# A hybrid decoder layer on one core: 128 bytes of padding behind the constants, and nine projections instead of eight in the second RWKV loop, the last of them behind the next stage's loads

## The chip, the core and the metric

The kernel runs on one core of one Trainium2 chip. The metric is the device time of one execution in microseconds, as the median of several runs. The core has five engines that run side by side, each with its own queue of instructions: TensorE (matmuls; PE in the profile, and PEld for its weight loads), VectorE (DVE), ScalarE (ACT), GpSimd (POOL) and SyncE (SP, which only issues DMAs here).

## What is computed

One layer (depth 1) over 1024 positions of width 1024, in float32. The normalised input goes through one projection of 3840 columns, and its columns feed three mixers side by side:

```
z = rmsnorm(h, norm_mix_g) @ w_in
h = h + concat[ hgrn2_mix (4 heads x 128), dilated_window_mix (4 heads x 64), rwkv7_mix (4 heads x 64) ] @ w_out
h = h + conv_glu_ffn(rmsnorm(h, norm_ffn_g), ffn_up, conv, ffn_down)          # d_ff 2816
h = h + sigmoid(rmsnorm(h, norm_ple_g) @ ple_gate) * (p @ ple_proj)
return rmsnorm(h, final_norm_g)
```

HGRN-2 is a gated recurrence with a decay per key channel, worked in chunks; the attention mixes three causal windows of dilation 1, 4 and 16; RWKV-7 is a delta-rule recurrence with its own decay, small gates and a group norm behind it.

## The kernel before, in words

Activations lie transposed, 128 channels on the partitions and 1024 positions along the free axis. A float32 matmul is made of three matmuls on a reduced 32-bit type: both operands are split into a high and a low part, and `mm3` (L139 to L143) issues high x high, high x low and low x high, for two halves of 512 positions. A weight block of 128 x 1024 is loaded by `load_w` (L107), cast to its high part on ScalarE (L116) and reduced to its low part on GpSimd or VectorE (L118). A projection of 128 columns of z is then 8 k blocks of 6 matmuls, 128x128 by 128x512.

There are 30 projections. Eight feed RWKV directly. The other 22 feed HGRN (columns 8 to 23) and attention (24 to 29); they are independent of RWKV and serve as cover for its small, dependent matmuls. Two generators make them:

- `project_rest` works in both RWKV loops. It yields after every k block, accumulates in a PSUM buffer of 1024 columns (tag dp, two buffers), scales it on VectorE (`finish`: L425, L428, L430) and stores the result to DRAM (L419). It asks for the weights of its next projection at k = 3.
- `project_late` works in the HGRN and attention stage. It yields after every half of 512 positions, accumulates in the smaller PSUM buffers (tag mx, four), finishes and stores each half (L448). When it has run out, it allocates the tiles for the split mixer outputs, in the memory of the split inputs.

The order of the 22 is one list, `js`: 8 to 15, 24, 25, 26, 16, 17, 20, 21, 19, 23, 27, 28, 29, 18, 22. `rwkv` runs the two pairs of RWKV heads after each other (p = 0, 1). Each time it takes the next projections from the list by FILL: the first number of a pair is how many are done ahead of the main loop, the second how many are taken in all. `rwkv_main` has 22 turns with one k block each. `rwkv_norm` then runs the group norm of the second half of positions: statistics on VectorE, ScalarE and GpSimd (L694 to L703), then transposes on TensorE (L710), the gate matmul (L714) and the gating on VectorE (L711, L712, which reads bv, L715). It has three steps, and takes up to 6 k blocks behind each. What is left of the generator is drained behind it. With FILL (4, 8) the second loop has 64 blocks: 32 ahead, 22 in the main loop, and 10 in the norm.

The RWKV tiles' memory is then given to the pools of the HGRN and attention stage, and `phase_mix` interleaves four generators there by an order written out by hand, 36 rounds: A (HGRN heads 0 and 2), B (heads 1 and 3, from round 6), C (attention, in the rounds of TURNS) and F (`project_late` with the four projections that are left, in odd rounds up to 15). The first step of A loads f and q of head 0 from DRAM (L458, SyncE's queue); the first step of C loads q, k and v of the first attention half (L458, GpSimd's queue). The attention scores (L1034) go to two dp buffers, one for each of two heads; the values' transposes (L1017) and HGRN's scores (L869, L890) go to mx buffers. The framework sets semaphores by itself, and lets an instruction go ahead of others in its engine's order where it expects its operands earlier.

Memory of the on-chip store is taken from two sides. The left side begins with the constants (parameters, `cst`, and `cmask`, the HGRN masks as one byte per entry, 9 masks x 128 = 1152 bytes per partition); behind them come small tiles, the weight tiles (tags whi, wlo) and then the stages' pools: x0 and x1 with the split activations, ty with three operand sets of the FFN, and others. The right side begins with a tile of 160 bytes that nobody uses (pool edge), then t16 (sixteen operand tiles of 2048 bytes: p1 and p2 of the up phase, the activations of the down phase), ep, px (the embedding's input), and in the last phase x0 (first half of the positions). The large tiles of both sides are whole multiples of 256 bytes, so what comes first on a side sets the place of all that follows, counted within 256 bytes.

The output projection, the FFN (a seven-product scheme for 2x2 blocks: up phase at L1189, 22 units of 7 products; down phase at L1483, 7 products over 11 k) and the last gate follow; the change touches no line of them.

Of the kernel before, what the change touches and what calls it, by code (L numbers as in the profile page):

```python
# [36 lines left out]

CC_ID, CC_BONE, CC_MSK, CC_I64 = 0, 128, 256, 384
NC0 = CC_HG = 448
NCC = CC_HG + 9 * 128  # L40


def shape_constants():
    c = np.zeros((P, NCC), np.float32)
    pp = np.arange(P)[:, None]
    ff = np.arange(P)[None, :]
    c[:, CC_ID:CC_ID + P] = pp == ff
    same = (pp // 64) == (ff // 64)
    c[:, CC_BONE:CC_BONE + P] = same
    f64 = np.arange(64)[None, :]  # L50
    c[:, CC_MSK:CC_MSK + 64] = pp % 64 < f64
    c[:, CC_MSK + 64:CC_MSK + 128] = pp % 64 <= f64
    c[:, CC_I64:CC_I64 + 64] = pp % 64 == f64
    c[:, CC_HG:CC_HG + P] = pp == ff
    for l in range(7):
        n = 1 << l
        c[:, CC_HG + (l + 1) * P:CC_HG + (l + 2) * P] = (pp // n) ^ 1 == ff // n
    c[:, CC_HG + 8 * P:CC_HG + 9 * P] = pp < ff
    u = np.arange(T)[None, :]
    d = pp - (u - 896)  # L60
    cnt = ((d >= 0) & (d <= 128)).astype(np.float64)
    cnt += (d >= 0) & (d <= 512) & (d % 4 == 0)
    cnt += (d >= 0) & (d <= 2048) & (d % 16 == 0)
    sw = np.where(cnt > 0, 8.0 * np.log(np.maximum(cnt, 1.0)), -1e30).astype(np.float32)
    return c, sw


def interleave(order, streams):

    live = dict(streams)  # L70
    while live:
        for s in order:
            if s in live and next(live[s], STOP) is STOP:
                del live[s]


def handover(a, b, steps=14):

    for _ in range(steps):
        next(a)  # L80
        yield
    for i, _ in enumerate(b):
        if i == 1:
            for _ in a:
                yield
        yield
# [5 lines left out]
class Trunk:  # L92
# [183 lines left out]
    def setup(self):  # L276
# [7 lines left out]
        self.id64 = self.cst[:, CC_I64:CC_I64 + 64]  # L284
        self.cmask = cp.tile([P, NCC - NC0], U8, name="cmask")
        few = cp.tile([P, 8], F32, name="few")
# [15 lines left out]
    def load_masks(self, tp):  # L302
        t = tp.tile([P, NCC - NC0], F32, name="ctmp")
        self.nc.gpsimd.dma_start(t, self.a["cst"][:, NC0:])
        self.nc.gpsimd.tensor_copy(self.cmask, t)
# [18 lines left out]
    def phase_mix(self):  # L324
        nc, tc = self.nc, self.tc
        self.mix_norm()
        with tc.tile_pool(name="slots", bufs=1) as slots:
            self.slots, self.NSLOT = slots, 8
            self.rwkv()
        self.O, self.done = None, []  # L330
        for p in (0, 1):
            self.o_split(6 + p)
        with tc.tile_pool(name="hg", bufs=1) as slots, tc.tile_pool(name="sw", bufs=1) as sp:
            self.slots, self.NSLOT = slots, 11
            self.hgrn_setup()
            self.sp = sp
            self.swmask = sp.tile([P, T], F32, name="swmask")
            nc.scalar.dma_start(self.swmask, self.a["swm"])
            A = handover(self.hgrn_head(0), self.hgrn_head(2))
            B = handover(self.hgrn_head(1), self.hgrn_head(3))  # L340
            order = []
            for r in range(36):
                order += "C" * (r in self.TURNS) + "A" + "B" * (r > 5) + "F" * (r % 2 and r < 16)
            interleave(order, {"A": A, "B": B, "C": self.swa(sp), "F": self.project_late(self.rest)})

    TURNS = [i * 33 // 22 for i in range(23)]

    def mix_norm(self):

# [122 lines left out]
    def rwkv(self):  # L472
        nc, tc = self.nc, self.tc
        lt = self.mix_in(0, 6, "lora")
        nc.scalar.activation(lt[0:64, :], lt[0:64, :], AF.Tanh)
        sg = self.mix_in(1, 7, "sg")
        nc.scalar.activation(sg, sg, AF.Sigmoid)
        self.z = {}
        js = iter((*range(8, 16), 24, 25, 26, 16, 17, 20, 21, 19, 23, 27, 28, 29, 18, 22))
        for p in (0, 1):  # L480
            d = {}
            with tc.tile_pool(name=f"pre{p}", bufs=1) as tp:
                self.rwkv_prep(p, tp, lt, d)
                self.rwkv_inverse(p, tp, d)
            lead, n = self.FILL[p]
            fill = self.project_rest([next(js) for _ in range(n)])
            for _ in range(8 * lead):
                next(fill)
            with tc.tile_pool(name=f"rk{p}", bufs=1) as rp:
                self.rwkv_main(p, rp, sg, d, fill)  # L490
            self.rwkv_norm(p, sg, d, 1, fill)
            for _ in fill:
                pass
        self.rest = list(js)

    FILL = (5, 10), (4, 8)

    def rwkv_prep(self, p, tp, lt, d):

# [172 lines left out]

    HALVES = tuple((slice(a, a + 32), slice(a + 32, a + 64)) for a in (0, 64))

    def rwkv_norm(self, p, sg, d, hf, fill):
        for _ in self.rwkv_norm_steps(p, sg, d, hf):
            for _ in range(6):
                next(fill, None)

    def rwkv_norm_steps(self, p, sg, d, hf):  # L680
# [1021 lines left out]
```

## Time and profile before

| | |
|---|---|
| runs of before, us | 1500.29, 1500.64, 1498.69; median 1500.29 |
| the profiled execution | 1501.27 us, of which the span from first to last instruction is 1499.5 |
| mean granted TensorE clock | 0.988 of full speed |
| HBM read, written | 119.95 MB, 46.40 MB (111 GB/s over the span) |
| matmuls on the page | 8910, with as many weight loads |

Times in a row are counted from the span's start. A row of the timeline has start, duration, engine, line, operation and operands; "x2" means that two of a kind were merged. A matmul's duration is modelled and overlaps with its follower's, so a stream's rate is read from start to start. The idle time in brackets is that of the engine just before the instruction, with what ended it.

### The profile page before, as it was taken

How to read it: one execution, taken by the hardware profiler on the slowest of the kernel's cores; microseconds unless marked ns; L12 is line 12 of the kernel's file. 1: busy time of each engine (PE TensorE's matmuls, PEld its weight loads, DVE VectorE, ACT ScalarE, POOL GpSimd, SP SyncE). 2: the span in 40 equal slices, each digit the busy share in tenths (PEclk: the TensorE clock that was granted, in tenths of full speed). 3: DMA queues.
4: the chain of work that ended last, by engine and by line, in shares of the span. 5: the costliest groups of instructions: out<-in, count | busy, mean ns of one | idle time of the engine just before them, and what ended most of it. 6: DMA issues, size and time to landing. Idle time of an engine off the chain costs nothing.

```text
span 1499.5 us, 22728 instructions
## 1 busy us (share of the span) xinstructions
PE 1444.2 (96%) x8910; PEld 1168.8 (78%) x8910; DVE 1062.3 (71%) x1556; ACT 593.2 (40%) x976; POOL 379.8 (25%) x276
## 2 busy tenths in 40 slices
PE   6999999999969999999999999999999999999996
PEld 5778878787857886878778888888888888887885
DVE  6486242782446588646879888888888799767685
ACT  6512221313214445425454444444444444455552
POOL 2221011200112132122034444445554000002332
PEclk9999999999979999999999999999999999999998
DMA  5124012131051211174323333333233883351343
GB/s 215 43 84 135 30 36 93 50 113 58 30 189 64 94 65 41 43 276 167 133 86 112 101 103 106 106 105 98 100 106 118 301 283 92 103 158 57 119 145 123
DMA packets 79739, 167.83 MB, mean 112 GB/s; under 512 B 19920, under 2 KB 22224, under 8 KB 79632
## 3 DMA queue, kind: packets, MB, share of 16 engines
q1 hardware_dynamic: 66176, 146.39, 29.5%
q10 hardware_dynamic: 12368, 15.99, 3.1%
q0 software_dynamic: 1088, 4.00, 0.7%
q8 instruction: 70, 1.15, 0.3%
q14 instruction: 37, 0.30, 0.1%
HBM read 119.95 MB, written 46.40 MB: 111 GB/s over the span
## 4 chain that ended last, share of the span: by engine, by line
PE 48%; issue 2%; DVE 1%; POOL 1%; ACT 0%; DMA 0%; POOLq 0%; ACTq 0%; DVEq 0%
PE bg L1189 15%; PE bv L1189 12%; PE bv L1483 7%; PE bg L1483 7%; PE bv L139 1%; PE bv L141 1%; PE bv L143 1%; PE dp L143 1%; PE dp L141 1%; PE dp L139 1%; PE bg L139 1%; PE bg L141 1%; PE bg L143 1%; POOL wlo L118 0%; POOL rst L192 0%
## 5 line engine op out<-in xcount | busy, mean ns | idle before, releaser
L139 PE MATMUL dp<-xh,whi 128*128 128x512 f32 x544 | 187.9, 404 | 9.4 <-ACT xh L380 9.2
L141 PE MATMUL dp<-xl,whi 128*128 128x512 f32 x544 | 182.5, 395 | 0.8 <-DVE xl L381 0.7
L143 PE MATMUL dp<-xh,wlo 128*128 128x512 f32 x544 | 182.3, 394 | 0.6 <-POOL wlo L118 0.6
L118 POOL TENSOR_TENSOR wlo<-wraw,whi 128x512 fp32r<-128x512 f32 x60 | 81.4, 1356 | 308.1 <-ACT whi L116 279.0
L118 POOL TENSOR_TENSOR wlo<-raw,whi 128x512 fp32r<-128x512 f32 x84 | 135.1, 1627 | 76.2 <-ACT whi L116 76.2
L116 ACT CAST whi<-wraw 128x512 fp32r<-128x512 f32 x120 | 73.3, 618 | 167.7 <-PE dp L141 118.5
L1189 PE MATMUL bg<-t,whi 128*128 128x512 f32 x352 | 135.4, 395 | 0.0
L139 PEld LDWEIGHTS dp<-xh,whi 128*128 128x128 f32 x544 | 99.4, 189 | 33.7 <-ACT xh L380 9.2
L141 PEld LDWEIGHTS dp<-xl,whi 128*128 128x128 f32 x544 | 101.8, 188 | 25.5 <-DVE xl L381 3.1
L143 PEld LDWEIGHTS dp<-xh,wlo 128*128 128x128 f32 x544 | 102.3, 189 | 23.4 <-issue 1.0
L118 POOL TENSOR_TENSOR wlo<-s,whi 128x512 fp32r<-128x512 f32 x44 | 64.4, 1464 | 175.8 <-ACT whi L116 175.8
L1483 PE MATMUL bg<-t,whi 128*128 128x512 f32 x308 | 97.2, 396 | 0.0
L1483 PE MATMUL bv<-t,whi 128*128 128x512 f32 x308 | 96.9, 395 | 0.0
L116 ACT CAST whi<-raw 128x512 fp32r<-128x512 f32 x88 | 52.5, 618 | 95.2 <-issue 48.7
L116 ACT CAST whi<-s 128x512 fp32r<-128x512 f32 x66 | 38.9, 619 | 123.9 <-PE bg L1189 116.1
L1189 PEld LDWEIGHTS bg<-t,whi 128*128 128x128 f32 x352 | 65.9, 187 | 15.8
L192 POOL TENSOR_TENSOR rst<-rst,mhalf 128x4 f32<-128x4 f32 (+1 forms) x9 | 10.3, 1148 | 249.2 <-DVE rst L188 231.6
L1483 PEld LDWEIGHTS bv<-t,whi 128*128 128x128 f32 x308 | 57.8, 188 | 14.0
L118 DVE TENSOR_TENSOR wlo<-wraw,whi 128x512 fp32r<-128x512 f32 x60 | 47.6, 796 | 29.8 <-ACT whi L116 25.1
L1483 PEld LDWEIGHTS bg<-t,whi 128*128 128x128 f32 x308 | 57.7, 188 | 13.9
L1189 PE MATMUL bg<-t,wlo 128*128 128x512 f32 x176 | 68.2, 395 | 0.0
L1479 ACT CAST t<-t 128x512 fp32r<-128x512 f32 x77 | 47.7, 620 | 50.1 <-PE bv L1483 30.4
(402 smaller groups left out, 3502.1 us busy)
## 6 DMA issues: line engine op xcount, KB each, us to landing
raw<-in_ffn_up_dram SPq DMA_DIRECT2D x44, 512.0 KB, 3.5
wraw<-in_w_in_dram SPq DMA_DIRECT2D x30, 512.0 KB, 3.5
z<-zst SPq DMA_DIRECT2D x18, 512.0 KB, 3.2
gb<-ct SPq DMA_DIRECT2D x33, 256.0 KB, 2.2
t<-gb SPq DMA_DIRECT2D x33, 256.0 KB, 2.8
t<-gt SPq DMA_DIRECT2D x33, 256.0 KB, 2.7
zl<-z SPq DMA_DIRECT2D x16, 512.0 KB, 4.0
wraw<-in_ple_gate_dram SPq DMA_DIRECT2D x16, 512.0 KB, 3.4
```

The source lines that it names most:

```text
L116: self.cast = nc.scalar.copy(hi, src).ins
L118: eng.tensor_tensor(lo, src, hi.bitcast(F32), ALU.subtract)
L139: nc.tensor.matmul(ps[hf], wh, xh[hf], start=first, stop=False)
L141: nc.tensor.matmul(ps[hf], wh, xl[hf], start=False, stop=False)
L143: nc.tensor.matmul(ps[hf], wl, xh[hf], start=False, stop=last)
L192: nc.gpsimd.tensor_tensor(r2, r, self.mhalf[:, :n], ALU.pow)
L1189: nc.tensor.matmul(ps, w[part == 2][:, s], X[k][part == 1], start=start and k == part == 0, stop=k == 3 and part == 2, skip_group_check=no ...
L1479: nc.scalar.copy(xh, x)
L1483: nc.tensor.matmul(ps[m], wt[part == 2][:, m * P:(m + 1) * P], (xh, xl)[part == 1], start=k == part == 0, stop=k == NK - 1 and part == 2)
```

## The change

There are two parts. The constants get a tenth block of 128 columns, which stays zero and is used by nobody: `cmask` becomes 1280 bytes wide, and so does the DMA and the cast that fill it.

The second RWKV loop takes nine projections instead of eight (28 comes over from the late ones), 72 blocks: 32 ahead, 22 in the main loop. Its norm takes 3 blocks behind each of its three steps instead of up to 6. The generator is not drained there any more. Its remaining 9 blocks (the last one of projection 27 and all of 28) are a stream M in the next stage, ahead of the rounds, behind the first steps of C and A, which are the loads. TURNS loses its first entry, since that step of C now stands ahead. F has three projections instead of four.

```diff
-NCC = CC_HG + 9 * 128
+NCC = CC_HG + 10 * 128
...
-            order = []
+            order = ["C", "A"] + ["M"] * 24
             for r in range(36):
                 order += "C" * (r in self.TURNS) + "A" + "B" * (r > 5) + "F" * (r % 2 and r < 16)
-            interleave(order, {"A": A, "B": B, "C": self.swa(sp), "F": self.project_late(self.rest)})
-
-    TURNS = [i * 33 // 22 for i in range(23)]
+            interleave(order, {"A": A, "B": B, "C": self.swa(sp), "F": self.project_late(self.rest), "M": self.more})
+
+    TURNS = [i * 33 // 22 for i in range(1, 23)]
...
-            self.rwkv_norm(p, sg, d, 1, fill)
-            for _ in fill:
-                pass
-        self.rest = list(js)
-
-    FILL = (5, 10), (4, 8)
+            self.rwkv_norm(p, sg, d, 1, fill, 6 - 3 * p)
+            if p == 0:
+                for _ in fill:
+                    pass
+        self.rest, self.more = list(js), fill
+
+    FILL = (5, 10), (4, 9)
...
-    def rwkv_norm(self, p, sg, d, hf, fill):
+    def rwkv_norm(self, p, sg, d, hf, fill, n):
         for _ in self.rwkv_norm_steps(p, sg, d, hf):
-            for _ in range(6):
+            for _ in range(n):
                 next(fill, None)
```

## The prediction, written before the result

> **What bounds the kernel now.** I read the page first, then who TensorE waited for, then the busy time by stretch around the end of the second RWKV loop.
>
> ```profile
> span 1499.5 us, 22728 instructions
> PE 1444.2 (96%) x8910; PEld 1168.8 (78%) x8910; DVE 1062.3 (71%) x1556; ACT 593.2 (40%) x976; POOL 379.8 (25%) x276
> ...
> PE 48%; issue 2%; DVE 1%; POOL 1%; ACT 0%; DMA 0%; POOLq 0%; ACTq 0%; DVEq 0%
> ```
>
> TensorE is busy 96% of the span, and nearly all of the traced part of the final chain is its own work. Time comes out of this kernel in two ways only: fewer holes in TensorE's row, or a shorter step from one matmul to the next.
>
> ```profile
> PE swq L1034 <- DMA zl<-z: 12.9, 1, 12.9
> PE dp L139 <- ACT xh L380: 9.2, 1, 9.2
> ```
>
> The longest wait (total, times, longest) is a single one: the first attention scores wait 12.9 us for loads. It lies where the second RWKV loop hands over to the HGRN and attention stage.
>
> ```profile
> 405.80:423.20 17.40, 17.40 (x104) 13.62 (x100) 8.81 (x13) 3.90 (x6) 2.90 (x2) 1.00 0.17 61
> 423.20:436.10 12.90, 0.02 (x3) 0.05 (x2) 2.84 (x5) 1.94 (x2) 2.26 (x4) 0.64 0.98 368
> 436.10:447.20 11.10, 10.74 (x37) 8.36 (x38) 7.09 (x18) 2.55 (x8) 1.07 (x2) 0.64 0.25 92
> 447.20:545.00 97.80, 96.88 (x669) 78.03 (x668) 65.64 (x118) 41.60 (x87) 22.40 (x17) 1.00 0.21 73
> 545.00:640.00 95.00, 88.08 (x690) 70.71 (x687) 71.86 (x142) 46.46 (x99) 23.84 (x19) 0.98 0.17 57
> ```
>
> Columns after the stretch: length, busy PE, PEld, DVE, ACT, POOL, granted clock, DMA share, GB/s. In the hole TensorE does 0.02 of 12.90 us while the DMA engines are 98% busy. The clock is 0.64 there and still 0.64 in the 11 us behind it. Up to 545, where projection halves lie between the heads' work, TensorE is idle 0.92 of 97.8 us; behind that, without them, 6.92 of 95.0.
>
> **The handover, part by part.** The rows around it:
>
> ```profile
> 405.81 0.73 PE L139 MATMUL dp<-xh,whi 128*128 128x512 f32 x2
> 411.42 0.69 DVE L703 TENSOR_TENSOR y<-y,gnr 128x512 f32<-128x512 f32 x1 [1.81 <-POOL gnr L702]
> 421.00 1.15 PE L710 MATMUL yt<-cst,y 64*64 64x64 f32 x32
> 421.11 1.22 DVE L425 TENSOR_TENSOR zst<-dp,rstd 128x1024 f32<-128x1024 f32 x1 [4.50 <-PE dp L143]
> 423.08 0.69 DVE L712 TENSOR_TENSOR oc<-oc,bv 128x512 f32<-128x512 f32 x1
> 423.84 2.76 SPq L458 DMA_DIRECT2D zl<-z  x4
> 424.32 1.73 POOL L458 DMA_DIRECT2D zl<-z  x3 [1.70 <-DVE oc L712]
> 436.08 0.80 PE L1034 MATMUL swq<-zl,zl 64*128 64x128 f32 x4 [12.88 <-DMA zl<-z]
> 440.00 0.78 PE L139 MATMUL zp<-xh,whi 128*128 128x512 f32 x1
> 443.99 0.40 PE L139 MATMUL zp<-xh,whi 128*128 128x512 f32 x1
> 447.44 1.95 PE L869 MATMUL hsc<-zl,hk 128*128 128x128 f32 x16
> ```
>
> Before: from 405.81 one fill block of the last loop turn, then ten within the closing norm (six, then four), 11 in all to 421.00: (421.00 - 405.81) / 11 = 1.38 us a block. Then the norm's transposes, the gate matmul, and nothing. The loads into the next stage's tiles start at 423.84, right after L712 has read bv (423.08 + 0.69), since they lie where the loop's tiles were.
>
> After: one block, then three, three, and the transposes at 405.81 + 7 x 1.38 = 415.5. Their operand is ready earlier (L703 ends at 412.11), so three blocks still cover that chain, with 3.4 us to spare. L712 moves as much, about 5.5 us, and with it the loads, on SP, on POOL's queue and the mask load on ACT's: they start near 418.3 and, as 436.08 - 423.84 = 12.2 us are needed, they are in by 430.5. TensorE has, from 415.5, the transposes and gate matmul (2.2 us, 421.00 to 423.20), three blocks (4.1) and the nine left over (12.4): until 434.2. So the loads hide with 3.7 us to spare, and the 12.9 us hole closes. What is late next is the attention's score buffer: the scores use the same two PSUM buffers as the projections, so the second head's waits for L425 of projection 28 (1.22 us). The value transposes and the first HGRN scores (1.95 us) need neither, so I charge 0.7, between 0 and 1.6. Z stores 27 and 28 now stand behind the heads' first loads on SP; 27 is wanted only by the second attention half.
>
> Without the hole the clock has no reason to drop. Between 440.00 and 443.99 nine matmul steps took 3.99 us, 0.443 each, against 0.227 in the warm rows further down: 1.9 us lost there, and the scores and transposes before it (436.08 to 440.00, also cold) at most 1.9 more: I take 3.0 in all.
>
> The work itself is only moved: the eight blocks of projection 28 replace two of the eight late halves.
>
> ```profile
> L448 SPq DMA_DIRECT2D z<-zst x8: 319/319/320, 448.4 to 544.7; - x8
> 0.00:20.00 20.00, 9.50 (x27) 5.85 (x28) 11.46 (x24) 14.37 (x26) 7.78 (x13) 1.00 0.92 329
> L305 POOL CAST cmask<-ctmp x1: 1168/1168/1168, 9.8 to 9.8; 128x1152 uint8<-128x1152 f32 x1
> ```
>
> With six halves the cover ends four rounds earlier. Some 20 us of the stage then run like the stretch behind 545 (7.3% idle) instead of like the one ahead (0.9%): 1.3 us, I take 1.5; the bound is 6, if VectorE (76% busy behind 545) leads. HGRN's first head runs one turn earlier against the rest; nothing.
>
> The wider mask costs 128 x 128 x 4 = 65.5 KB at the start, where DMA is 92% busy at 329 GB/s: 0.2 us. L305 grows by a ninth, 0.13 us on POOL beside it.
>
> Handover in all: -12.9 - 3.0 + 0.7 + 1.5 + 0.2 = -13.5 us. Bounds: -12.9 - 1.9 + 1.6 + 6 + 0.2 = -7 and -12.9 - 3.8 + 0.2 = -16.5.
>
> **The places.** The steps of three streams of the same 128x512 matmul, each by its first and last row:
>
> ```profile
> 659.77 0.39 PE L139 MATMUL dp<-xh,whi 128*128 128x512 f32 x1
> 667.93 0.39 PE L139 MATMUL dp<-xh,whi 128*128 128x512 f32 x1
> ...
> 899.76 0.40 PE L1189 MATMUL bg<-t,whi 128*128 128x512 f32 x1
> 904.82 0.40 PE L1189 MATMUL bg<-t,wlo 128*128 128x512 f32 x1
> ...
> 1200.37 0.63 PE L1483 MATMUL bv<-t,whi 128*128 128x512 f32 x2
> 1205.50 0.63 PE L1483 MATMUL bg<-t,whi 128*128 128x512 f32 x2
> ```
>
> 36 steps in 8.16 us are 0.2267 each; 22 in 5.06 are 0.2300; 22 in 5.13 are 0.2332. Nothing waits in any of them, and the clock is 1.0. What differs is where the moving operand lies. From the kernel's tile sizes, every matmul operand of the left pools (weight pieces, x0 and x1 of the mix, ty) now starts 192 bytes past a multiple of 256, as the mask is 4.5 x 256 bytes; the right pools (t16, px, x0 of the last phase) start 64 past one, through the 160-byte edge tile. In the first stream both operands are on the left, in the third all moving ones (named t) are on the right, in the second every other one.
>
> ```profile
> L1189 PE MATMUL bg<-t,whi 128*128 128x512 f32 x352 | 135.4, 395 | 0.0
> L1189 PE MATMUL bg<-tp3h,whi 128*128 128x512 f32 x88 | 34.3, 389 | 1.7 <-ACT whi L116 1.7
> L1483 PE MATMUL bg<-t,whi 128*128 128x512 f32 x308 | 97.2, 396 | 0.0
> ```
>
> Within one phase the right operand's mean is 395 ns and the left one's 389. With 128 bytes more, everything on the left moves to 64 as well, weights and moving operands, and the right stays. My forecast is that the distance counts, not the place itself: a matmul's read and the next one's weight read run at the same time,
>
> ```profile
> 444.70 0.39 PE L139 MATMUL zp<-xh,whi 128*128 128x512 f32 x1
> 444.70 0.19 PEld L141 LDWEIGHTS zp<-xl,whi 128*128 128x128 f32 x1
> ```
>
> so the two addresses can get in each other's way, and left with left, both moved alike, keeps its 0.2267. Then the right operands fall to it too. The down phase has 7 products x 11 k x 12 = 924 matmuls, all with right operands: 924 x 0.0065 = 6.0 us. In the up phase 2 of the 7 products of a unit (p1, p2) have right operands, 22 x 2 x 12 = 528, and such a pair loses 2 x 0.0033: 528 x 0.0066 = 3.5. Eight embeddings of 12 and the first half of the last gate, 8 x 24, are 288 x 0.0065 = 1.9, an estimate by the down phase's step. In all -11.4 us; if the distance counts, the bounds are -9 (the 288 bring nothing) and -13 (0.01 us of error on a row's start, at both ends, is 0.001 a step); it is 0 if something else about the right pools counts, and the other sign is below.
>
> The sum: -13.5 - 11.4 = -24.9. The profiled execution took 1501.27 us, about 1.0 above the median of 1500.29, so 1476.4 there and 1475.5 as median.
>
> **The rivals.** *The place itself counts*: a moving operand at 64 costs 6.5 ns wherever its weights lie. For it: the three streams fit this just as well, since the weights lie at 192 in all of them. Against it: it has no part for the weight read that runs alongside. Then the left matmuls, (30 projections + 8 outputs) x 48 + 192 of the last gate + 22 x 5 x 12 of the up phase = 3336, all become slow: +21.7, nothing on the right gains, and the time is 1500.3 - 13.5 + 21.7 = 1508.5. It decides from 13.5 / 3336 = 4.0 ns a matmul on.
>
> By the Trainium skill (page "TensorE: Matmul & The Clock Gate", Part 2, step by step) the tensor engine reads moving operand and weights through two independent ports, and loading the next weights takes no read bandwidth from the running matmul. By that rule a distance between them can't matter, and this rival or the next would hold; no run here shows two long streams with the same distance and different places.
>
> *Only the handover pays*: the right operands stay slow for a reason that the shift leaves alone. For it: all of them are in pools allocated late and in the same part of memory. Then 1486.8.
>
> *The hole is only shared out*: the nine blocks run, but the first scores still wait, or the stage is led by VectorE and gives the time back behind 545 (71.86 of 95.0 busy). Against it: TensorE is idle under 1% up to 545. Then the handover brings some 3, and with the places 1486.
>
> **How the numbers follow.** The runs of before spread over 1.95 us, so about 0.2% (3 us) can be told from no change. Forecast 0.65; the place itself 0.12; only the handover 0.13; the hole shared out 0.08; both parts failing at once 0.02. The forecast's own range is 1500.3 - 16.5 - 13 = 1471 to 1500.3 - 7 - 9 = 1484; with the two cases at 1486 and 1486.8 and their spread it becomes 1469 to 1490, which leaves out the slow rival. Faster 0.86, same 0.02, slower 0.12.
>
> **What would show it.** Right: no wait of the scores on a load; the transposes near 415.5, loads near 418, the granted clock 1.0 through the handover; L448 six times; 0.2267 per step in the up and down phases and for right and left operands one mean. The place rival would show 0.233 in the projections and the output phase. I am wrong if TensorE's idle time behind 430 grows by more than 6 us, or if the down phase keeps 0.2332.

## The result and the profile after

| | us | runs |
|---|---|---|
| before | 1500.47 (1498.69 to 1500.73) | 4 |
| after | 1488.85 (1486.37 to 1489.02) | 4 |
| forecast | 1475.5 (1469 to 1490) | |

The ratio of after to before is 0.9921, with a 95% interval of 0.9904 to 0.9938. So the change saves 11.6 us where 25 were forecast. The profiled execution of after took 1488.94 us. From line 492 on, a line of after has a number higher by one than in before.

The page of after, first its span and busy times, then the two groups of part 5 that answer to those of before (instructions, busy us, mean ns of one, idle time ahead of them):

```profile
span 1487.2 us, 22736 instructions
PE 1437.7 (97%) x8910; PEld 1172.1 (79%) x8910; DVE 1066.6 (72%) x1555; ACT 594.5 (40%) x976; POOL 379.8 (26%) x276
...
L1190 PE MATMUL bg<-t,whi 128*128 128x512 f32 x352 | 133.2, 389 | 0.0
...
L1484 PE MATMUL bg<-t,whi 128*128 128x512 f32 x308 | 95.1, 390 | 0.0
```

The two groups went from 395 and 396 ns to 389 and 390: the places did what was forecast of them. Two rows of one stream of the down phase give the step from start to start; "..." leaves out 14 rows, each of two matmuls:

```profile
1200.25 0.62 PE L1484 MATMUL bg<-t,wlo 128*128 128x512 f32 x2
...
1207.05 0.62 PE L1484 MATMUL bv<-t,whi 128*128 128x512 f32 x2
```

Between them lie 30 steps in 6.80 us, 0.2267 each, where before had 0.2332.

Now the handover. The same stretches as before, with the same columns (length, busy PE, PEld, DVE, ACT, POOL, clock, DMA share, GB/s):

```profile
405.80:423.20 17.40, 17.40 (x135) 14.05 (x132) 9.25 (x12) 3.16 (x5) 4.62 (x5) 1.00 0.31 96
423.20:436.10 12.90, 12.90 (x62) 10.65 (x61) 10.03 (x16) 3.05 (x6) 3.37 (x3) 1.00 0.99 399
436.10:447.20 11.10, 9.62 (x43) 8.13 (x43) 5.33 (x10) 3.50 (x8) 2.54 (x3) 0.85 0.45 145
447.20:545.00 97.80, 91.21 (x644) 72.99 (x643) 66.80 (x121) 43.03 (x92) 23.30 (x18) 0.97 0.19 65
545.00:640.00 95.00, 89.39 (x668) 70.14 (x667) 71.23 (x139) 46.12 (x94) 20.40 (x16) 0.98 0.15 51
```

The hole of 12.9 us is gone: TensorE is busy in all of 423.2 to 436.1 while the DMA engines load at 99%. But in 447.2 to 545 its idle time rose from 0.92 to 6.59 us, and the clock there is no longer full. The waits of TensorE say the same (total, times, longest):

```profile
PE swt L1058 <- ACT ob L1072: 3.7, 1, 3.7
...
PE swt L1058 <- DVE zst L425: 1.7, 1, 1.7
...
PE swq L1035 <- DVE zst L425: 1.5, 1, 1.5
```

No wait of the scores on a load is left. New are two waits of the attention's transposes (L1058), of 3.7 and 1.7 us, and the second head's scores wait 1.5 us for L425, as forecast in kind. The timeline has both places. First the handover:

```profile
416.57 1.15 PE L711 MATMUL yt<-cst,y 64*64 64x64 f32 x32
...
419.79 0.80 SPq L458 DMA_DIRECT2D zl<-z  x2
...
435.92 0.49 PE L1035 MATMUL swq<-zl,zl 64*128 64x128 f32 x2
```

The transposes lie 1.1 us behind the forecast 415.5 and the loads 1.5 us behind 418.3; the whole program up to there was 1.0 us later than before (the first transposes of the norm lie up to 3.4 us apart in the profiles of the kernels here). Then the new hole:

```profile
514.97 0.39 PE L143 MATMUL zp<-xh,wlo 128*128 128x512 f32 x1
515.29 1.99 PE L1035 MATMUL swq<-zl,zl 64*128 64x512 f32 x8
516.24 2.29 DVE L968 TENSOR_TENSOR ho<-ho,hrs 128x1024 f32<-128x1024 f32 x1 [1.78 <-POOL hrs L966]
518.45 2.22 DVE L849 TENSOR_SCALAR zl<-zl,olb,lb 128x1024 f32<-128x1024 f32 x1
521.32 0.66 PE L1058 MATMUL swt<-cst,lg 128*128 128x128 f32 x4 [1.67 <-DVE zst L425]
522.98 1.21 DVE L1042 CUSTOM_DVE_ANT_0 lg<-swq,swmask 128x1024 f32<-128x1024 f32 x1
524.24 1.15 ACT L1044 ACTIVATE lg<-lg,sden 128x1024 f32<-128x1024 f32 x1 [7.87 <-DVE sden L1042]
525.39 0.25 ACT L1072 COPY ob<-swo 128x128 f32<-128x128 f32 x1
525.69 0.90 PE L1058 MATMUL swt<-cst,lg 128*128 128x128 f32 x3 [3.71 <-ACT ob L1072]
```

Read it from below. TensorE waits for an mx buffer, which the copy L1072 on ScalarE frees. The copy itself is ready, but stands in ScalarE's order behind the exponential L1044, which waits 7.87 us for the score reduction L1042 on VectorE. And L1042 stands in VectorE's order behind the end of HGRN's head 0 (L968) and the start of head 2 (L849 and its followers), 516.24 to 523. I call that stretch of VectorE the change of heads. The scores came to L1042 only then because the last late half ran right ahead of them, until 514.97. Where it all lies, 520 to 530 us:

```profile
520.00:530.00 10.00, 4.97 (x24) 3.67 (x26) 8.50 (x16) 4.11 (x8) 1.31 (x3) 0.73 0.55 185
```

TensorE is idle half of the time, and the clock is 0.73. In before the same reduction (L1041 there) ran at 514.0 and the change of heads only from 526.7, beside a late half:

```profile
514.04 1.23 DVE L1041 CUSTOM_DVE_ANT_0 lg<-swq,swmask 128x1024 f32<-128x1024 f32 x1 [0.38 <-PE swq L1034]
...
526.61 0.47 PE L139 MATMUL zp<-xh,whi 128*128 128x512 f32 x1
526.67 0.81 DVE L848 TENSOR_SCALAR zl<-zl,olb,lb 128x1024 f32<-128x1024 f32 x1
```

### The profile page after: what moved, and what is told of

Its sections match the earlier page's. It is cut to its first block, busy times and chain, and to the rows that moved or that the text cites. A ratio compares the mean times of both kernels' runs of the same rounds, so it can differ in the third digit from the quotient of the medians.

```text
span 1487.2 us, 22736 instructions
## 1 busy us (share of the span) xinstructions
PE 1437.7 (97%) x8910; PEld 1172.1 (79%) x8910; DVE 1066.6 (72%) x1555; ACT 594.5 (40%) x976; POOL 379.8 (26%) x276
## 4 chain that ended last, share of the span: by engine, by line
PE 48%; issue 2%; DVE 1%; POOL 1%; DMA 0%; ACT 0%; POOLq 0%; ACTq 0%; DVEq 0%
PE bg L1190 15%; PE bv L1190 12%; PE bv L1484 7%; PE bg L1484 7%; PE bv L139 1%; PE dp L143 1%; PE bv L143 1%; PE bv L141 1%; PE dp L139 1%; PE dp L141 1%; PE bg L139 1%; PE bg L143 1%; PE bg L141 1%; POOL wlo L118 0%; DMA out_dram<-ot 0%
## 5 line engine op out<-in xcount | busy, mean ns | idle before, releaser
L139 PE MATMUL dp<-xh,whi 128*128 128x512 f32 x560 | 193.5, 405 | 9.9 <-ACT xh L380 9.7
L143 PE MATMUL dp<-xh,wlo 128*128 128x512 f32 x560 | 187.0, 394 | 0.8 <-POOL wlo L118 0.8
L141 PE MATMUL dp<-xl,whi 128*128 128x512 f32 x560 | 187.3, 395 | 0.4 <-DVE xl L381 0.3
L118 POOL TENSOR_TENSOR wlo<-wraw,whi 128x512 fp32r<-128x512 f32 x60 | 83.0, 1383 | 314.0 <-ACT whi L116 287.8
L118 POOL TENSOR_TENSOR wlo<-raw,whi 128x512 fp32r<-128x512 f32 x84 | 134.7, 1623 | 76.2 <-ACT whi L116 76.2
L1190 PE MATMUL bg<-t,whi 128*128 128x512 f32 x352 | 133.2, 389 | 0.0
L139 PEld LDWEIGHTS dp<-xh,whi 128*128 128x128 f32 x560 | 102.4, 189 | 35.3 <-ACT xh L380 9.7
L141 PEld LDWEIGHTS dp<-xl,whi 128*128 128x128 f32 x560 | 104.8, 189 | 25.6 <-DVE xl L381 2.8
L143 PEld LDWEIGHTS dp<-xh,wlo 128*128 128x128 f32 x560 | 105.5, 189 | 24.3 <-POOL wlo L118 1.2
L118 POOL TENSOR_TENSOR wlo<-s,whi 128x512 fp32r<-128x512 f32 x44 | 63.9, 1452 | 173.7 <-ACT whi L116 160.0
L1484 PE MATMUL bg<-t,whi 128*128 128x512 f32 x308 | 95.1, 390 | 0.0
L118 DVE TENSOR_TENSOR wlo<-wraw,whi 128x512 fp32r<-128x512 f32 x60 | 47.4, 792 | 30.1 <-ACT whi L116 25.4
```

The source lines that it names most:

```text
L118: eng.tensor_tensor(lo, src, hi.bitcast(F32), ALU.subtract)
L139: nc.tensor.matmul(ps[hf], wh, xh[hf], start=first, stop=False)
L141: nc.tensor.matmul(ps[hf], wh, xl[hf], start=False, stop=False)
L143: nc.tensor.matmul(ps[hf], wl, xh[hf], start=False, stop=last)
L1190: nc.tensor.matmul(ps, w[part == 2][:, s], X[k][part == 1], start=start and k == part == 0, stop=k == 3 and part == 2, skip_group_check=no ...
L1484: nc.tensor.matmul(ps[m], wt[part == 2][:, m * P:(m + 1) * P], (xh, xl)[part == 1], start=k == part == 0, stop=k == NK - 1 and part == 2)
```

## The experiments

Differences are against the runs of before on the same chip.

### The places

**The padding alone** is before with one line changed:

```diff
-NCC = CC_HG + 9 * 128
+NCC = CC_HG + 10 * 128
```

> Before with the wider mask alone, so all left operands move from 192 to 64 past a multiple of 256. If the distance between moving operand and weights counts: steps of 0.2267 us in the down phase, and 10 to 11 us faster than before (the changed kernel gained 3.2 in the up phase, 6.1 in the down phase and 1.1 behind it). If the place itself counts, the projections slow down to 0.233 a step, and the sum is slower by 10 or more. If the gains of the changed kernel in these phases come from its other order, no change.

Measured: 1491.04 us against 1500.45, ratio 0.9942 (0.9929 to 0.9954). That is 9.4 us from a block of constants that nobody reads. The mean of the down phase is the one of after, and the left operands, which now lie at 64 as well, did not slow down. The second line is that of the output projections between 640 and 745 us, the same here as in before:

```profile
L1483 PE MATMUL bg<-t,whi 128*128 128x512 f32 x308 | 95.2, 390 | 0.0
...
L139 PE MATMUL dp<-xh,whi 128*128 128x512 f32 x116 | 43.6, 391 | 0.0
```

**The handover alone** is after with nine masks:

```diff
-NCC = CC_HG + 10 * 128
+NCC = CC_HG + 9 * 128
```

> The changed kernel with the narrow mask of before, so only the handover is changed. If the two parts add up: 1 to 2 us faster than before, as the hole of 6 us behind 519 us and the longer cold clock give most of the 13 us back. If the handover brings what was forecast, and padding spoils something in the stage, 10 us or more. If the new holes are an accident of the padded kernel, they are gone here.

Measured: 1497.38 against 1500.45, ratio 0.9981 (0.9972 to 0.9990): 3.1 us, where 13.5 were forecast. Its trace has the same hole at 519 us and the same wait:

```profile
PE swt L1058 <- ACT ob L1072: 3.7, 1, 3.7
```

So the two parts add up (9.4 + 3.1 = 12.5, measured 11.6), and the shortfall lies in the handover.

**The other side moved** is before with the edge tile at 288 bytes instead of 160. The left side stays at 192, and the right operands come to 192 as well:

```diff
-            e(self.pool("edge", side="right")).tile([P, 40], F32, name="edge")
+            e(self.pool("edge", side="right")).tile([P, 72], F32, name="edge")
```

> Before with an edge tile of 288 bytes instead of 160, so that the right operands move to 192, where the left ones are. If only the distance counts: the same gain as with the padding, 10 to 11 us, and 0.2267 a step in the down phase. If the padding gains because 64 is the better place for weights or anything else on the left, no change or a loss here.

Measured: 1490.11 against 1500.45, ratio 0.9929 (0.9916 to 0.9943). The gain is the same within 1 us, with both operands at 192 here and at 64 with the padding. The two runs together show that the distance between moving operand and weights counts, and neither of the two places.

```profile
L1483 PE MATMUL bg<-t,whi 128*128 128x512 f32 x308 | 95.2, 390 | 0.0
```

**The table of places** is a kernel of its own, 16 streams of 48 matmuls. Its core, with weights at w and the moving operand at m, counted within 256 bytes:

```
for w in (192, 64):
    for m in (0, 32, 64, 96, 128, 160, 192, 224):
        for i in range(48):
            nc.tensor.matmul(ps, wts[:, at(w) + i % 4 * 128 ...], mov[:, at(m) ...])
```

> A kernel of its own that leaves out the whole layer: 16 streams of 48 matmuls 128x512 of the same reduced type, weights 192 or 64 past a multiple of 256, moving operand at 0, 32, ... 224 past one. If the distance counts: step 0.2267 where both are alike, 0.233 at a distance of 128, and the two rows of the table are the same up to a shift by 128. If the place of the moving operand counts: the two rows are the same without a shift. If two independent reads never meet: one step everywhere.

Measured, mean step from start to start in ns:

| weights at | m 0 | 32 | 64 | 96 | 128 | 160 | 192 | 224 |
|---|---|---|---|---|---|---|---|---|
| 192 | 229.2 | 233.5 | 233.2 | 234.3 | 233.4 | 233.2 | **227.2** | 233.4 |
| 64 | 233.3 | 233.2 | **227.2** | 233.4 | 229.1 | 233.6 | 233.4 | 234.1 |

The second row is the first one moved by 128, as the weights are. Four streams in the timeline, each 48 matmuls with its start and duration:

```profile
40.25 11.36 PE L35 MATMUL w192m64z<-mov,wts 128*128 128x512 f32 x48
...
85.09 11.07 PE L35 MATMUL w192m192z<-mov,wts 128*128 128x512 f32 x48
...
129.59 11.07 PE L35 MATMUL w64m64z<-mov,wts 128*128 128x512 f32 x48
...
173.91 11.36 PE L35 MATMUL w64m192z<-mov,wts 128*128 128x512 f32 x48
```

The moving operand at 64 is slow with weights at 192 and fast with weights at 64. No place is slow by itself.

### The handover

**Other rounds for the late halves.** After, with F in other rounds and nothing else:

```diff
-"F" * (r % 2 and r < 16)
+"F" * (r in (1, 4, 7, 10, 12, 14, 16))
```

> The changed kernel with the six late projection halves in rounds 1, 4, 7, 10, 12 and 14 instead of 1 to 11. If the hole of 6 us behind 519 us is there because TensorE has no cover left in rounds 12 to 15: it closes, the cold clock behind it too, and the kernel is 5 to 8 us faster than the changed one (about 1482). If the RWKV outputs' splits on ACT, DVE and POOL make it: they move along to round 16, and some hole stays there. If it is the heads' start one round ahead, no change (1489).

Measured: 1478.75 against 1500.07, ratio 0.9855 (0.9839 to 0.9871), 10 us under after. The stretch 447.2 to 545 of it:

```profile
447.20:545.00 97.80, 94.32 (x696) 76.48 (x694) 72.08 (x140) 47.04 (x102) 26.14 (x20) 1.00 0.20 70
```

Idle time is 3.48 us instead of 6.59, and the clock is full there; behind it, from 545 to 640, it is 0.96 (0.98 in after). The six halves are the same; only their rounds differ, and that of the generator's end, its seventh step.

**The same without the padding**, against the kernel with those other rounds:

```diff
-NCC = CC_HG + 10 * 128
+NCC = CC_HG + 9 * 128
```

> The kernel after with the six late halves spread over rounds 1, 4, 7, 10, 12, 14 and 16 (as in the run that closed the hole at 519 us), but with nine masks instead of ten, so without the padding. It tells what the handover is worth by itself when its cover reaches far enough. If the two parts of the change simply add, it is the spread kernel's 1478.75 us plus the 9.4 us that the padding alone brought: 1488 us, 12 us under the kernel before, which is near the 13.5 forecast for the handover. If the spread kernel's gain needs the padding (a faster stream there shifting the work against the clock), it stays above 1492 us.

Measured: 1487.60 against 1500.84, ratio 0.9913 (0.9898 to 0.9927): 13.2 us from the handover alone. That is near the forecast 13.5, but in another kernel than the one for which it was made.

**The splits behind the last half.** When `project_late` ends, it splits finished mixer outputs (L162, L164), and in after that pass on GpSimd (516.2 to 519.7) lies beside the change of heads. Two empty steps ahead of it were to move it:

```diff
                 yield
+        yield
+        yield
         self.O = self.xall()
```

> The changed kernel with two empty steps before the late generator's end, so that the output tiles and the RWKV outputs' splits stand behind the stage's order, as in the kernel before, and not in round 13. If the splits fill VectorE and GpSimd at the head change and so make the hole: it shrinks to under 2 us and the kernel is 4 to 8 us faster than the changed one. If missing cover makes it: the hole stays and the time is that of the changed kernel within 2 us.

Measured: 1486.76 against 1500.07, ratio 0.9914 (0.9897 to 0.9930); the hole stays (waits of 1.7 and 3.7 us; the expectations count such gaps from start to start of two matmuls, 1.9 and 4.0). It is a weak test: L164 still ran beside the end of head 0, at 519.04, so the edit did not move it away. The next run answers in part.

**As many late halves as before.** The last projection goes back to the late ones, so eight halves run, until 547:

```diff
-            self.rwkv_norm(p, sg, d, 1, fill, 6 - 3 * p)
+            self.rwkv_norm(p, sg, d, 1, fill, 6 - 4 * p)
...
-    FILL = (5, 10), (4, 9)
+    FILL = (5, 10), (4, 8)
```

> The changed kernel with eight projections in the second loop, two blocks behind each step of the norm and the last four behind the next loads, so that eight late halves stay as cover. From the changed kernel's rows the loads need 15 us from the transposes on and the cover there is 2.2 + 6 x 1.36 = 10.4, so a wait of 4 to 5 us on a load; no hole behind 519. If missing cover is what gave the gain back: 1483 to 1486. If the hole has another cause and stays: 1492 or more.

Measured: 1497.20 against 1500.07, ratio 0.9980 (0.9970 to 0.9989). A miss, and a useful one. The first transposes wait 7.7 us for a load, where 4 to 5 were expected, since six blocks behind the norm's transposes cover less than twelve; but the hole at 517 us is there too, in the middle of the halves:

```profile
PE vt L1018 <- DMA zl<-z: 7.7, 1, 7.7
PE swt L1058 <- ACT ob L1072: 3.7, 1, 3.7
```

My theory until then was that the cover ends too early. It falls here: halves ran at 505.3 to 512.6 and at 529.1, and the hole opened between them. No split of the mixer outputs runs there, but another pass on GpSimd does (L118, 2.24 us from 513.10), and beside it L849 takes 2.23 us instead of 0.81. So a pass on GpSimd beside the change of heads is not ruled out as a part of the cause. The order is that of after: a half, the scores, and L968 and L849 on VectorE ahead of L1042.

```profile
512.53 1.99 PE L1035 MATMUL swq<-zl,zl 64*128 64x512 f32 x8
512.99 1.22 DVE L968 TENSOR_TENSOR ho<-ho,hrs 128x1024 f32<-128x1024 f32 x1 [1.78 <-POOL hrs L966]
514.13 2.23 DVE L849 TENSOR_SCALAR zl<-zl,olb,lb 128x1024 f32<-128x1024 f32 x1
...
518.68 1.21 DVE L1042 CUSTOM_DVE_ANT_0 lg<-swq,swmask 128x1024 f32<-128x1024 f32 x1
```

**The heads a round later:**

```diff
-order += "C" * (r in self.TURNS) + "A" + "B" * (r > 5) + "F" * (r % 2 and r < 16)
+order += "C" * (r in self.TURNS) + "A" * (r > 0) + "B" * (r > 5) + "F" * (r % 2 and r < 16)
```

> The changed kernel with the first HGRN chain back in step with the rest (its second step in round 1, not 0). If the shift of one round brings the head change onto the attention's longest turns and so makes the hole: it goes, 4 to 8 us faster than the changed kernel. If cover or splits make it: it stays, within 2 us of the changed kernel.

Measured: 1488.72 against 1500.07, ratio 0.9924 (0.9909 to 0.9939), as after. The scores are now reduced at 516.2, ahead of the change of heads, which starts at 528.1, and the waits for L1072 are 0.6 us at most. But TensorE waits 5.2 us at another place (5.46 from start to start): head 1's next product (L891) waits for L896, which is queued behind L968.

```profile
528.13 0.81 DVE L849 TENSOR_SCALAR zl<-zl,olb,lb 128x1024 f32<-128x1024 f32 x1
...
533.92 2.05 PE L891 MATMUL hsc<-qt,ks 128*128 128x128 f32 x8 [5.19 <-DVE qt L896]
```

This is the place where before had a late half, at 526.61. Here the halves have run out by then, so with the heads' turn put back it is the missing half that shows.

**Halves still farther apart:**

```diff
-"F" * (r % 2 and r < 16)
+"F" * (r in (1, 5, 9, 12, 15, 18, 21))
```

> The kernel after with the six late halves still farther apart, in rounds 1, 5, 9, 12, 15, 18 and 21, so that the last lies near 565 us. Theory (cover must lie beside every stretch in which the heads and the attention alone leave TensorE idle): the stretch behind 545 us gets some of it, but the same six halves leave more of the stretch ahead of it bare; nothing at 519 us, small gaps all along, 1476 to 1484 us, near the spread kernel's 1478.75. Rival (the hole at 519 us came from which round a half stands in, not from how far the cover reaches): a hole of 4 us or more with a half clock comes back, and the time is 1486 us or more.

Measured: 1483.13 against 1500.84, ratio 0.9882 (0.9865 to 0.9898). No hole at 519; the scores are reduced at 503.3, and a half runs at 507.8 beside the change of heads. Smaller gaps come back elsewhere (a wait of 2.7 us that ends at 558), and the clock is 0.95 from 545 to 640.

**One half moved**, the sixth, from round 11 to 13:

```diff
-"F" * (r % 2 and r < 16)
+"F" * (r in (1, 3, 5, 7, 9, 13, 15))
```

> The kernel after with a single late half moved: the sixth comes in round 13 instead of 11. In the runs so far the hole lies where the first HGRN head gives way to the third (VectorE runs L968, L849, L852 and L854, some 7 us in all, ahead of the next score reduction) and no late half runs on TensorE beside it: in after the sixth half ends at 515.0 us and the change runs from 516.2; where a half lies over the change (before, 526.6; the two spread kernels, 511.2 and 507.8) there is no hole. Theory of the uncovered change: the sixth half moves to 515 to 525 us, the gaps of 1.9 and 4.0 us there and the half clock behind them go, and the time falls by 4 to 8 us to 1481 to 1485 us. Rival (the amount and the spread of all six halves count): with one half moved and five in place a hole of 3 us or more stays, and the time is 1487 us or more.

Measured: 1480.54 against 1499.61, ratio 0.9874 (0.9860 to 0.9889), 8.3 us under after (7.5 when each is taken against before on its own chip). Its timeline at the place of the hole:

```profile
510.54 1.98 PE L1035 MATMUL swq<-zl,zl 64*128 64x512 f32 x6
...
513.49 1.22 DVE L1042 CUSTOM_DVE_ANT_0 lg<-swq,swmask 128x1024 f32<-128x1024 f32 x1
...
515.89 0.24 ACT L1072 COPY ob<-swo 128x128 f32<-128x128 f32 x1
...
516.31 0.81 DVE L849 TENSOR_SCALAR zl<-zl,olb,lb 128x1024 f32<-128x1024 f32 x1
```

The scores are made 4.75 us sooner, as no half stands ahead of them, and L1042 and L1072 are through before the change of heads begins. The half itself went to 523.8, behind the change, not beside it as expected: by these rows, what counted was that it no longer stood ahead of the scores. One thing moved along: the generator's end goes from round 13 to 15, and with it the split on GpSimd (L164) from 516.2 to 529.7. Without it L968 and L849 take 1.23 and 0.81 us instead of 2.29 and 2.22. How much of the gain is due to that was not tried. From 520 to 530, and the whole stretch:

```profile
520.00:530.00 10.00, 9.57 (x64) 8.38 (x65) 7.29 (x17) 4.43 (x12) 2.57 (x3) 1.00 0.01 2
...
447.20:545.00 97.80, 94.68 (x684) 75.77 (x682) 68.50 (x132) 46.40 (x101) 25.48 (x20) 1.00 0.19 65
```

Against after the stretch has 3.5 us less idle time (3.12 instead of 6.59). The half clock there is gone and so is that up to 640: 97.8 x 0.03 + 95 x 0.02 = 4.8 us, more than the waiting itself.

**Heads and half later.** The kernel of the heads a round later, with the sixth half in round 14:

```diff
-"A" * (r > 0) + "B" * (r > 5) + "F" * (r % 2 and r < 16)
+"A" * (r > 0) + "B" * (r > 5) + "F" * (r in (1, 3, 5, 7, 9, 14, 15))
```

> The kernel after with the HGRN heads 0 and 2 one round later, as in the run before of that kind, where the change of heads moved to 528.1 us and left a gap of 5.46 us (1488.72 us), and with the sixth late half moved from round 11 to 14. Theory of the uncovered change: the half moves to 522 to 532 us, beside the change, the gap of 5.46 us falls under 2 us, and the time comes to 1481 to 1485 us. Rival (the amount and the spread of the halves count): the gap stays above 3 us and the time is 1487 us or more.

Measured: 1489.11 against 1499.61, ratio 0.9932 (0.9916 to 0.9949). A miss: the wait of 5.2 us is unchanged, now from 519.6 on. The half came to 526.5, behind the product that waits, where it covers nothing:

```profile
521.38 2.07 DVE L968 TENSOR_TENSOR ho<-ho,hrs 128x1024 f32<-128x1024 f32 x1 [1.56 <-POOL hrs L966]
...
524.81 2.05 PE L891 MATMUL hsc<-qt,ks 128*128 128x128 f32 x8 [5.19 <-DVE qt L896]
```

Taken together: the change of heads keeps VectorE for some 7 us, and what is queued behind it comes late. If that is the reduction L1042 (after, and the runs with eight halves and with the splits), TensorE waits 3.7 us for L1072, and 1.7 us more in two of them; if it is L896 with no half ahead of L891 in TensorE's order (the two runs with the heads later), 5.2 us; if L1042 is through by then (the runs with other rounds), no gap as long is left there.

## Why the prediction was right and wrong

**The places: right.** Forecast -11.4, measured alone -9.4, and by the traces of before and after: the up phase took 3.2 us less (forecast 3.5), the down phase 6.1 less (6.0), what lies behind it 1.0 less (1.9; this term was too large, and why is open). The rival of the place itself and that of the handover alone have fallen, the first by the table and by the padding alone, which put the left operands to 64 and did not slow them, the second by the padding alone. By the Trainium skill (page "TensorE: Matmul & The Clock Gate", Part 2, step by step) two independent ports feed the array, and a weight load takes no bandwidth from the running matmul. The table disagrees by 6 ns in 233 for a stream that loads weights for each matmul; the measurement decides. Why the two reads get in each other's way is not shown, and a stream that keeps its weights was not tried.

**The handover's hole: right.** 12.9 us of idle time became none, the transposes moved as worked out, and the loads hid behind the moved blocks. The scores' wait for L425 was 1.5 us, forecast 0.7 within 0 to 1.6.

**What failed** are two sentences on the work behind it: "With six halves the cover ends four rounds earlier ... I take 1.5", and "HGRN's first head runs one turn earlier against the rest; nothing." Neither holds, and each is enough for a gap. The earlier turn put the change of heads, in before at 526.7 us and beside a half, to 516.2, where a half stood ahead of the scores; with eight halves the wait of 3.7 us is there all the same. With the turn put back, the change lies at 528.1, but the half that before had beside it is missing, TensorE waits 5.2 us, and the time stays (1488.72). The stretch 447.2 to 545 lost 5.7 us, not 1.5, and 1.3 came back up to 640. What a pass on GpSimd adds beside the change stays open. I had worked with the mean idle share of a stretch (7.3% against 0.9%); the loss is a single place where the orders of three engines cross. My bound of 6 held for the idle time, but for the wrong reason (VectorE leading behind 545: there TensorE's idle time fell from 6.92 to 5.61).

**The clock: wrong by sign, and the largest miss.** I took -3.0, as "without the hole the clock has no reason to drop". Length times one minus the granted clock gives for before 11.1 x 0.36 + 95 x 0.02 = 5.9 us, and for after 11.1 x 0.15 + 97.8 x 0.03 + 95 x 0.02 = 6.5 up to 640. And the output phase, which the change doesn't touch, had a dip in after alone, the first of these rows before's, the second after's:

```profile
640.00:745.00 105.00, 103.12 (x465) 84.13 (x463) 68.83 (x103) 45.50 (x76) 20.62 (x16) 1.00 0.52 188
```

```profile
640.00:745.00 105.00, 101.92 (x452) 83.32 (x451) 68.86 (x104) 46.62 (x75) 19.78 (x15) 0.98 0.52 186
```

That is 105 x 0.02 = 2.1 us more, 2.7 in all instead of -3.0. So 5.7 of the 10.4 us between the forecast and the measured handover are the clock. The step that failed is the quoted sentence: much shorter waits than the hole were followed by a half clock. The scores' wait of 1.5 us, which ends at 438.30, is one (0.85 in 436.1 to 447.2), and before's own row up to 640 has another (0.98). The dip in the output phase stands in every run with the handover changed, except the two with rounds 1, 4, 7, 10, 12, 14 and 16; why is open.

The sum for the handover, from the stretches: hole -12.9, the 11 us behind it +1.1, up to 545 +5.7, up to 640 -1.3, up to 745 +1.2, clock +2.7: -3.5, against -3.1 measured. With other rounds for the same halves it is -13.2.

Of my two signs of being wrong one came true in substance: counted from 436.1, behind the old hole, TensorE's idle time grew by 6.7 us up to 745 (1.1 + 5.7 - 1.3 + 1.2), and the step of the down phase fell as forecast. The case "only the handover pays" came nearest in time (1486.8), and that is luck: the places paid, and the handover brought 3.1. The case "the hole is only shared out" (1486) had both sizes nearly right, some 3 and the places, with the wrong mechanism: the scores did not wait for loads, and nothing was given back behind 545. The measured 1488.85 lies in the range of 1469 to 1490 only since that was widened for these two cases; the forecast's own range ended at 1484.

## What to carry to other kernels

Work that is moved ahead of interleaved streams shifts them against each other: follow the next long stretch of each engine, and see what is queued behind it on that engine and on the engines that wait for it, instead of charging a mean idle share. Charge the half clock that may follow each new wait, too. A block of cover helps only ahead of the waiting instruction in TensorE's order, and hurts where it delays the one that feeds the chain; moving one such block by two rounds, with the generator's end behind it, was worth some 8 us here, and the best rounds tried, with the whole change, give 1478.75 us. In long streams of 128x512 matmuls, let moving operand and weights begin at the same place within 256 bytes.

## What the runs showed of the hardware

- The step of a matmul stream that changes weights each time is 227.2 ns at distance 0 of the two operands within 256 bytes, 229.1 to 229.2 with the moving operand 64 bytes further, and 233.2 to 234.3 at the other six distances tried, 128 among them. Steps finer than 32 bytes were not tried.
- A short wait can be enough for the half clock. In after, a single wait of 1.48 us ends at 438.30, and the granted clock is 0.50 from 439.3 to 442.7; in the handover alone a wait of 1.3 us at the same place left it at 1.00. Behind the hole at 519 to 525.7 us, with waits of 1.7 and 3.7 us, 520 to 530 ran at a mean of 0.73. In the traces the half clock lasts 3.41, 6.83 or 10.24 us after waits of up to 8 us; around a hole of 12.9 us it lasted 17.07 in before and 13.65 in the run with the wider edge tile.
- One pass on VectorE had different lengths: L849 took 0.81 us, but 2.22 in after, where a pass of 3.47 us ran on GpSimd beside it (L164), and 2.23 with eight halves, beside a pass of 2.24 us (L118). That the one slows the other was not tried by itself.
